# Half-size block products at the end of each MLP chunk, and their sums moved to GpSimd

## The chip, the core and the metric

The kernel runs on one core of a Trainium2 chip. The metric is the device time of one execution in microseconds (us), median of the runs shown; smaller is better. The profile calls the engines PE (TensorE matmuls), PEld (TensorE weight loads), DVE (VectorE), ACT (ScalarE), POOL (GpSimd) and SP (SyncE, which here issues nearly all DMAs).

## The reference

Two layers of a residual network on 1024 tokens of 1024 features. Each layer is a mixing part (a gated delta rule in layer 0, attention in layer 1), an MLP, and a gated projection. The change lies in the MLP:

```
hn = rms_norm(h, ln_mlp[layer])
h = h + jnp.square(jax.nn.relu(hn @ w_mlp1[layer])) @ w_mlp2[layer]
```

`w_mlp1` is 1024 x 4096 and `w_mlp2` 4096 x 1024, all float32. "First product" is `hn @ w_mlp1`, "second product" the one with `w_mlp2`.

## The kernel before

**Matmuls.** Every float32 operand is split in two parts of a reduced format, hi (an ACT cast) and lo (raw minus hi, one DVE `tensor_tensor`), by `split`, profile lines L224 and L225. `mm3` makes one product of three matmuls: hi·hi, hi·lo, lo·hi. All go through `Ordered.matmul`, L78. The weight block is the stationary side (128 x 128), the activations the moving side, up to 512 columns (half the tokens).

**First product.** The 4096 hidden features are cut into 8 chunks of 512. A chunk is a 2 x 2 block product (512 inputs twice, 256 features twice, 512 tokens twice), made as seven block products instead of eight, with sums of blocks before and after (Winograd's form of Strassen's method). Each block product is `product`: two raw weight tiles are split, then 2 x 4 x 3 = 24 matmuls of 512 columns. `front(c)` makes two of the seven, `rest(c)` five, in this order: weight blocks a21 with t3, a11 with t2, a22 with t4, s1 with t1, and last a12 with b22. t1 to t4 and b22 are sums and parts of the normalized activations, made once in each layer by `operands`, `make_t4` and `make_t1`: DVE sums (L283), ACT casts, DVE lo parts. The last block product adds onto the PSUM tiles that s1·t1 left (`ps`), after DVE has read them for g22; then g12 = u + ps. The fronts of chunks 0 to 3 come ahead of `operands`; `rest(c)` is followed by `front(c + 2)` for c = 2 to 5, so chunks 0, 1, 6 and 7 have no front behind them.

**After it.** ACT makes relu and square (L349, L350). The second product is made by the same method and needs sums of g11 to g22: before the change six DVE operations at the end of each chunk (g2 = g11 + g12, then g22 - g2 and g21 - g2, each for two tiles). `save` writes seven arrays of the chunk to DRAM (`gd`), from where the second product (`product2`) loads them.

**Tiles.** Raw weight tiles come from a ring of 8 (`raw`), split weight tiles from a ring of 12 (`w`), PSUM tiles for products from 8 banks in turn.

**Order.** The kernel's text gives priorities; a scheduler then sets the order on each engine with its own timeline of the program, and each engine executes its queue strictly in that order. So instructions of neighbouring products can stand interleaved, and an instruction that waits holds up all behind it on its engine.

Of the kernel before, what the change touches and what calls it, by code (L numbers as in the profile page):

```python
# [11 lines left out]
F32 = mybir.dt.float32  # L12
F32R = mybir.dt.float32r
# [103 lines left out]
class Trunk:  # L117
# [157 lines left out]

    def mlp(self, x, x_tags, gain, w1, w2, gain_next, h_dram, p, last):
        nc = self.nc
# [4 lines left out]
        def tt(out, a, b, op):  # L282
            nc.vector.tensor_tensor(out, a, b, op)  # L283
            return out

        def large(tags):
            hi, lo = (self.slot(t, [P, 4, HT], F32R, "t") for t in tags)
            return [(hi[:, k], lo[:, k]) for k in range(4)]

        def operands():  # L290
# [20 lines left out]
            def make_t1():  # L311
                b22.extend(self.split(x22[k], *self.hs_parts(1, 4 + k)) for k in range(4))
                return [self.split(t1s[k], *t) for k, t in enumerate(large((x_tags[0][1], x_tags[1][1])))]

# [113 lines left out]
        if self.unsquared:  # L428
            for i, a in enumerate(self.unsquared):
                self.add_square(1, a, marks[i // 4])  # L430

            def sums():
# [4 lines left out]
            front(1, amid=sums)  # L437
            self.pe.floor = self.pe.mark
# [143 lines left out]
    def split_p(self, p):  # L582
# [1452 lines left out]
def trunk(tc, x, p, ln_mix_e, w_in_e, gmlp_v_gain, gmlp_ws, gmlp_bs, gdn_conv, gdn_a_log, gdn_dt_bias, gdn_out_gain,  # L2035
          w_out_e, ln_mix_o, w_qkv_o, attn_q_gain, attn_k_gain, diff_lambda, attn_sub_gain, w_out_o, ln_mlp, w_mlp1,
          w_mlp2, ln_ple, w_ple_gate, w_ple_proj, masks, out):
    with ExitStack() as ctx:
# [54 lines left out]
        for layer in range(2):  # L2093
# [68 lines left out]
```

## Time and profile before

| | |
|---|---|
| median of 3 runs | 2481.62 us (2481.59 to 2485.3) |
| span of the profiled execution, first to last instruction | 2479.0 us (no other time of that execution is listed; the median is 2.6 us above it) |
| busy share PE / PEld / DVE / ACT / POOL | 99% / 85% / 75% / 52% / 13% |
| granted TensorE clock | 1.000 |
| first products of the MLPs | about 450 to 782 us (layer 0) and about 1725 to 2060 us (layer 1) |

"Busy" is the time in which an engine had an instruction in work. A row of the timeline gives start, duration, engine, line, operation, result and operands, shape, and in brackets the idle time before it with what ended it. A row of the windows gives a stretch of the span and in it the busy time of PE, PEld, DVE, ACT and POOL with instruction counts, the granted clock, the DMA share and GB/s. A row of the groups gives all instructions of one line and shape: busy time, mean ns of one, idle time before them.

### The profile page before, as it was taken

To read this page: it belongs to the slowest core of one execution; us is meant where nothing else is said; L and a number is where in the kernel's file an instruction comes from. 1 tells how busy PE (TensorE), PEld (TensorE's weight loads), DVE (VectorE), ACT (ScalarE), POOL (GpSimd) and SP (SyncE) were. 2 spreads that over 40 slices of the span, in tenths; PEclk is the share of its full clock that TensorE was granted. 3 is DMA by queue.
4 is the path that set the end of the run, shared out by engine and by line. 5 is a ranking of instruction groups with operands and counts; after the bars stand their busy time and mean duration, and the time that the engine had idled before them with its cause. 6 is when DMAs were issued, how large, how long until landed. Compare 5 with 4: busy or idle time off the path is not lost.

```text
span 2479.0 us, 39877 instructions
## 1 busy us (share of the span) xinstructions
PE 2463.4 (99%) x13597; PEld 2103.6 (85%) x13597; DVE 1863.9 (75%) x3638; ACT 1289.7 (52%) x2593; POOL 316.8 (13%) x296
## 2 busy tenths in 40 slices
PE   9999999999999999999999999999999999999999
PEld 7898898888888887888899999988878888878887
DVE  7787776697676879566568888876886677788687
ACT  6543444565445434454366666664755455445543
POOL 0221221000000000000244443441000000000010
PEclk9999999999999999999999999999999999999999
DMA  8475645457557756553347776787475558657872
GB/s 252 121 247 124 179 150 164 141 194 235 162 176 256 242 179 198 187 172 111 115 109 165 165 168 154 192 223 236 140 232 189 177 187 283 212 184 218 230 246 87
DMA packets 537748, 458.55 MB, mean 185 GB/s; under 512 B 228932, under 2 KB 399176, under 8 KB 537544
## 3 DMA queue, kind: packets, MB, share of 16 engines
q1 hardware_dynamic: 507192, 450.75, 59.7%
q10 hardware_dynamic: 29584, 3.68, 1.0%
q8 instruction: 107, 1.75, 0.3%
q0 software_dynamic: 768, 1.57, 0.2%
q14 instruction: 97, 0.79, 0.1%
HBM read 321.51 MB, written 134.37 MB: 184 GB/s over the span
## 4 chain that ended last, share of the span: by engine, by line
PE 94%; DVE 2%; DMA 2%; ACT 1%; issue 1%; POOL 0%; SPq 0%; DVEq 0%; ACTq 0%; POOLq 0%
PE mm L78 83%; PE po L78 3%; PE qk L78 3%; PE aux L78 2%; PE tr L81 1%; DMA spill<-early 0%; DMA aT<-a_dram 0%; PE pz L78 0%; DVE w L225 0%; PE pvn L78 0%; DMA diag<-early 0%; PE py L78 0%; PE aux L81 0%; PE pks L78 0%; PE pkq L78 0%
## 5 line engine op out<-in xcount | busy, mean ns | idle before, releaser
L78 PE MATMUL mm<-g,w 128*128 128x512 f32 x2592 | 603.5, 394 | 1.3 <-DVE g L225 0.7
L224 ACT CAST w<-raw 128x512 fp32r<-128x512 f32 x598 | 364.6, 616 | 444.1 <-PE mm L78 368.2
L78 PEld LDWEIGHTS mm<-g,w 128*128 128x128 f32 x2592 | 486.2, 188 | 116.3 <-DVE g L225 1.6
L78 PE MATMUL mm<-hi,w 128*128 128x512 f32 x1728 | 551.3, 396 | 0.0
L78 PE MATMUL mm<-w,hi 128*128 128x256 f32 (+2 forms) x2528 | 502.5, 294 | 0.7 <-ACT t L1587 0.7
L225 DVE TENSOR_TENSOR w<-raw,w 128x512 fp32r<-128x512 f32 (+1 forms) x510 | 348.2, 690 | 161.4 <-ACT w L224 150.1
L78 PEld LDWEIGHTS mm<-w,hi 128*128 128x128 f32 x2528 | 401.0, 188 | 15.5 <-ACT t L1587 0.9
L78 PEld LDWEIGHTS mm<-hi,w 128*128 128x128 f32 x1728 | 323.8, 188 | 73.4
L78 PE MATMUL mm<-w,lo 128*128 128x256 f32 (+2 forms) x1264 | 367.7, 292 | 0.0
L78 PE MATMUL mm<-lo,w 128*128 128x512 f32 x864 | 340.0, 394 | 0.0
L78 PE MATMUL mm<-t,w 128*128 128x512 f32 x1152 | 270.6, 394 | 0.2 <-DVE t L225 0.2
L78 PEld LDWEIGHTS mm<-t,w 128*128 128x128 f32 x1152 | 216.2, 188 | 51.3 <-DVE t L225 1.1
L78 PEld LDWEIGHTS mm<-w,lo 128*128 128x128 f32 x1264 | 237.8, 188 | 5.8
L78 PEld LDWEIGHTS mm<-lo,w 128*128 128x128 f32 x864 | 162.5, 188 | 36.3
L224 ACT CAST g<-graw 128x512 fp32r<-128x512 f32 x216 | 132.7, 617 | 44.6 <-DMA graw<-gd 16.3
L225 DVE TENSOR_TENSOR g<-graw,g 128x512 fp32r<-128x512 f32 x216 | 147.4, 687 | 10.2 <-DMA gd<-g 7.3
L1069 ACT ACTIVATE lg<-lg,nm 128x384 f32<-128x384 f32 (+7 forms) x128 | 99.2, 775 | 82.6 <-DVE nm L1066 81.8
L265 POOL TENSOR_TENSOR r<-ms,mhalf 128x4 f32<-128x4 f32 x12 | 12.5, 1043 | 940.2 <-DVE ms L263 915.8
L225 POOL TENSOR_TENSOR w<-raw,w 128x512 fp32r<-128x512 f32 (+1 forms) x88 | 113.8, 1313 | 133.3 <-ACT w L224 93.4
L349 ACT ACTIVATE g<-g 128x512 f32<-128x512 f32 x96 | 60.5, 631 | 112.3 <-DVE g L283 102.4
L1066 DVE CUSTOM_DVE_ANT_0 lg<-qk,al 128x512 f32<-128x512 f32 (+3 forms) x128 | 74.4, 585 | 25.0 <-PE qk L78 21.1
L78 PE MATMUL mm<-ohi,w 128*128 128x512 f32 x256 | 87.4, 402 | 1.5 <-ACT ohi L1142 1.1
(340 smaller groups left out, 3534.9 us busy)
## 6 DMA issues: line engine op xcount, KB each, us to landing
raw<-in_w_mlp_dram SPq DMA_DIRECT2D x352, 256.0 KB, 3.5
graw<-gd SPq DMA_DIRECT2D x224, 256.0 KB, 2.9
gd<-g SPq DMA_DIRECT2D x192, 256.0 KB, 3.2
raw<-in_w_ple_gate_dram SPq DMA_DIRECT2D x76, 256.0 KB, 3.7
acc<-h_dram SPq DMA_DIRECT2D x64, 256.0 KB, 4.3
keep<-in_w_mlp_dram SPq DMA_DIRECT2D x64, 256.0 KB, 4.5
raw<-in_w_in_e_dram SPq DMA_DIRECT2D x60, 256.0 KB, 3.8
h_dram<-acc SPq DMA_DIRECT2D x48, 256.0 KB, 2.2
```

Of the source, the lines that this page charges most:

```text
L78: self._next(self.engine.matmul(*a, **k))
L81: self._next(self.engine.transpose(*a, **k))
L224: self.nc.scalar.copy(hi, src)
L225: (lo_engine or self.nc.vector).tensor_tensor(lo, src, f32(hi), ALU.subtract)
L265: nc.gpsimd.tensor_tensor(r, ms, self.mhalf[:, 0:4], ALU.pow)
L349: nc.scalar.activation(g, src, AF.Relu)
L1066: nc.vector.tensor_tensor_reduce(out=lg[:, k0:k1], in0=ps[:, : k1 - k0], in1=al[:, u0 + k0 : u0 + k1], scale=-1.0, scalar=3.0e38 if c == 0 ...
L1069: nc.scalar.activation(lg[:, :n], lg[:, :n], AF.Exp, bias=nm[:, r, nch - 1 : nch], scale=-1.0, accum_out=me.sums[:, b, r : r + 1])
```

## The change

The last block product of each chunk, a12·b22, is now itself made by the seven-product method on halves (256 inputs, 128 features, 256 tokens): `blocks`. Seven half-size products of 2 x 3 matmuls with 256 columns, 42 matmuls, take the place of 24 with 512 columns.

- Sums of the weight block (s12, s4 and a new half of a0): four POOL operations on 256 elements, in two more tiles of the raw ring; then four splits (three of 512 columns, one of 256) instead of two.
- Sums of b22, once in each layer: y1 to y4, four POOL operations of 512 columns, ahead of the other operands; their lo parts on POOL as well (two of 256 columns, three of 512), their casts on ACT.
- Four of the seven products go to two PSUM tiles of their own (p16, and p57 in halves); DVE adds them to u (four additions of 256 columns, two of 512, one operand in PSUM); the others add onto `ps` as before. The second product into p16 adds onto the first, after DVE has read it.
- The six sums for the second product at the end of each chunk move from DVE to POOL, in place of g12, so the first waits until g12 has been saved.
- The four raw tiles of `split_p` come from the raw ring instead of the pool `tmp`.

```
-    def mlp(self, x, x_tags, gain, w1, w2, gain_next, h_dram, p, last):
+    def mlp(self, x, x22s, x_tags, gain, w1, w2, gain_next, h_dram, p, last):
+        def sums(out, a, b, op):
+            nc.gpsimd.tensor_tensor(out, a, b, op)
+            return out
+        L, R = slice(0, 256), slice(256, 512)
...
+            sums(y1, x22s[:, k1, R], x22s[:, k1, L], ALU.subtract)
+            sums(y2, x22s[:, k2, R], y1, ALU.subtract)
+            sums(y3, x22s[:, k2, R], x22s[:, k1, R], ALU.subtract)
+            sums(y4, x22s[:, k2, L], y2, ALU.subtract)
+            for k in range(2):
+                self.split(y1[:, k], *(y[:, R] for y in b22[k]), nc.gpsimd)
...
+        def blocks(raws, b, ps, u):
+            a0, a1 = raws
+            lo, hi = slice(0, P), slice(P, 2 * P)
+            s12, s4 = self.raw(2, 256), self.raw(2, P)
+            sums(s12[:, :, lo], a0[:, :, hi], a1[:, :, hi], ALU.add)
+            sums(a0[:, :, hi], a0[:, :, lo], a0[:, :, hi], ALU.subtract)
+            sums(s12[:, :, hi], s12[:, :, lo], a0[:, :, lo], ALU.subtract)
+            sums(s4, a1[:, :, lo], s12[:, :, hi], ALU.subtract)
+            a0, a1, s12, s4 = (self.parts(x, nc.vector) for x in (a0, a1, s12, s4))
...
+            sub(p16, a0, lo, b[1, 1], True)
+            tt(u0[:, L], u0[:, L], p16, ALU.add)
+            sub(ps[0][:, L], a1, lo, b[2, 1])
+            sub(ps[1][:, L], a1, hi, b[4])
+            sub(p5, s12, lo, b[1], True)
+            for x in u:
+                tt(x[:, R], x[:, R], p5, ALU.add)
+            sub(p16, s12, hi, b[2])
+            tt(u0[:, R], u0[:, R], p16, ALU.add)
+            tt(u1, u1, both(p16), ALU.add)
+            sub(p7, a0, hi, b[3], True)
+            tt(u1, u1, both(p7), ALU.add)
+            sub(ps[0][:, R], s4, slice(0, P), b[2, 2])
...
-            product(a12, b22, ps)
+            blocks(a12, halves, ps, u)
...
-                tt(g2[i], g11[i], g12[i], ALU.add)
-            save(6, c, g2)
+                sums(g12[i], g11[i], g12[i], ALU.add)
+            save(6, c, g12)
-                tt(g22[i], g22[i], g2[i], ALU.subtract)
-                tt(g21[i], g21[i], g2[i], ALU.subtract)
+                sums(g22[i], g22[i], g12[i], ALU.subtract)
+                sums(g21[i], g21[i], g12[i], ALU.subtract)
```

What stands on the engines. First POOL, from the end of layer 0's mixing part on (r is the norm's factor, al belongs to the attention of layer 1, hundreds of us later). Before:

```order
L1900 TENSOR_TENSOR fo_5236<-so_5231,mhalf 128x4
L1906 TENSOR_TENSOR qkv_2530<-qkv_2530,qkv_701 128x4x128
L265 TENSOR_TENSOR r_5175<-ms_5173,mhalf 128x4
L265 TENSOR_TENSOR r_5796<-ms_5794,mhalf 128x4
L920 IOTA al_12490 128x1024
L921 AFFINE_SELECT al_12490<-al_12490 128x1024
```

Now (y are the sums of b22, lo their parts, raw_6372 is s12, raw_6366 a0 and raw_6373 s4 of chunk 0):

```order
L265 TENSOR_TENSOR r_5796<-ms_5794,mhalf 128x4
L287 TENSOR_TENSOR y_1074_6115<-acc_5498 128x512
L225 TENSOR_TENSOR lo_6108<-y_1074_6115,hi_6107 128x256
L225 TENSOR_TENSOR lo_6110<-y_1074_6115,hi_6109 128x256
L287 TENSOR_TENSOR y_6116<-acc_5498,y_1074_6115 128x512
L287 TENSOR_TENSOR y_6117<-acc_5498 128x512
L287 TENSOR_TENSOR y_6118<-acc_5498,y_6116 128x512
L287 TENSOR_TENSOR raw_6372<-raw_6366,raw_6368 128x2x128
L287 TENSOR_TENSOR raw_6366<-raw_6366 128x2x128
L287 TENSOR_TENSOR raw_6372<-raw_6372,raw_6366 128x2x128
L287 TENSOR_TENSOR raw_6373<-raw_6368,raw_6372 128x256
L225 TENSOR_TENSOR y_6313<-y_6116,y_6312 128x512
```

POOL had nothing to do during the first product; it now has thirteen operations at its start, two of which follow the last row shown. Next DVE at the end of chunk 0 (u and g as above, v is there g2, w are lo parts of weight blocks, s the sum s1). Before:

```order
L283 TENSOR_TENSOR g_6107<-u_5705,mm_6310 128x512
L283 TENSOR_TENSOR v_6115<-g_5707,g_6107 128x512
L225 TENSOR_TENSOR w_6518<-raw_6427,w_6517 128x512
L283 TENSOR_TENSOR g_6111<-g_6111,v_6115 128x512
L283 TENSOR_TENSOR g_6109<-g_6109,v_6115 128x512
L283 TENSOR_TENSOR g_6108<-u_5706,mm_6311 128x512
L225 TENSOR_TENSOR w_6558<-s_1141_6420,w_6557 128x512
```

Now:

```order
L283 TENSOR_TENSOR u_5705<-u_5705,mm_6394 128x256
L225 TENSOR_TENSOR w_6504<-raw_6483,w_6503 128x512
L283 TENSOR_TENSOR u_5705<-u_5705,mm_6395 128x256
L283 TENSOR_TENSOR u_5706<-u_5706,mm_6395 128x256
L283 TENSOR_TENSOR raw_6661<-raw_6661,raw_6491 128x512
L225 TENSOR_TENSOR w_6536<-raw_6489,w_6535 128x512
L225 TENSOR_TENSOR w_6540<-raw_6491,w_6539 128x512
L225 TENSOR_TENSOR w_6574<-raw_6485,w_6573 128x512
L283 TENSOR_TENSOR u_5705<-u_5705,mm_6394 128x256
L283 TENSOR_TENSOR u_5706<-u_5706,mm_6394 128x512
L283 TENSOR_TENSOR g_6127<-u_5705,mm_6332 128x512
```

The sums v and g - v are gone from DVE, the additions of PSUM tiles to u have come, with the splits of the next chunk's blocks between them. Last PE at the same place: mm_6310 (before) and mm_6332 (now) are `ps`, mm_6394 is p16, mm_6395 p57, mm_6447 and mm_6507 belong to the next chunk's first product. Before:

```order
L78 MATMUL mm_6448<-lo_6083,w_6443 128x512
L78 MATMUL mm_6310<-hi_6276,w_6350 128x512
L78 MATMUL mm_6310<-lo_6277,w_6350 128x512
L78 MATMUL mm_6310<-hi_6276,w_6351 128x512
L78 MATMUL mm_6310<-hi_6280,w_6350 128x512
```

Now:

```order
L78 MATMUL mm_6395<-hi_6109,w_6387 128x256
L78 MATMUL mm_6507<-hi_6068,w_6499 128x512
L78 MATMUL mm_6507<-lo_6069,w_6499 128x512
L78 MATMUL mm_6508<-hi_6068,w_6499 128x512
L78 MATMUL mm_6508<-lo_6069,w_6499 128x512
L78 MATMUL mm_6332<-hi_6111,w_6382 128x256
L78 MATMUL mm_6332<-lo_6112,w_6382 128x256
L78 MATMUL mm_6332<-hi_6111,w_6383 128x256
```

Matmuls of 256 columns have taken the place of those of 512, and products of the next chunk stand between them.

More of the change, by code (lines that the diff above doesn't have):

```diff
@@ L311, in make_t1 @@
             def make_t1():
[L312 to L313 removed]
+                for k in range(4):
+                    cols = slice(0, 256 if k < 2 else 512)
+                    self.split(x22[k][:, cols], *(y[:, cols] for y in b22[k]))
+                out = [self.split(t1s[k], *t) for k, t in enumerate(large((x_tags[0][1], x_tags[1][1])))]
+                halves.update({(1, 1): [[y[:, L] for y in b22[k]] for k in (0, 1)], (2, 1): [[y[:, L] for y in b22[k]] for k in (2, 3)],
+                               (2, 2): [[y[:, R] for y in b22[k]] for k in (2, 3)], 1: [[y[:, R] for y in b22[k]] for k in (0, 1)]})
+                for n, y in ((2, y2), (3, y3), (4, y4)):
+                    if n < 4:
+                        ys = [self.tp.tile([P, 2, 256], F32R, tag="t", name=self.nm("y")) for _ in range(2)]
+                    else:
+                        ys = [self.sp.tile([P, 2, 256], F32R, tag=t, name=self.nm("y"), bufs=1) for t in ("sqs1", "rb1")]
+                    self.split(y, *ys, nc.gpsimd)
+                    halves[n] = [[z[:, k] for z in ys] for k in range(2)]
+                return out
             return t3, t2, make_t4, make_t1
@@ L343, in product, with sub, both @@
             return ps
+        def blocks(raws, b, ps, u):
[7 more added lines that the diff above has]
+            a0, a1, s12, s4 = (self.parts(x, nc.vector) for x in (a0, a1, s12, s4))
+            p16, p57 = (self.mm_ps() for _ in range(2))
+            p16, p5, p7 = p16[:, L], p57[:, L], p57[:, R]
+            def sub(out, w, cols, y, new=False):
+                for k in range(2):
+                    self.mm3(out, [z[:, k, cols] for z in w], y[k], new and k == 0, k == 1, not new)
+            def both(p):
+                return p.unsqueeze(1).to_broadcast([P, 2, 256])
+            u0, u1 = u
+            sub(p16, a0, lo, b[1, 1], True)
+            tt(u0[:, L], u0[:, L], p16, ALU.add)
+            sub(ps[0][:, L], a1, lo, b[2, 1])
+            sub(ps[1][:, L], a1, hi, b[4])
+            marks.append(self.pe.mark)
+            sub(p5, s12, lo, b[1], True)
+            for x in u:
+                tt(x[:, R], x[:, R], p5, ALU.add)
+            sub(p16, s12, hi, b[2])
+            u1 = u1.rearrange("p (h t) -> p h t", h=2)
+            tt(u0[:, R], u0[:, R], p16, ALU.add)
[3 more added lines that the diff above has]
+            sub(ps[0][:, R], s4, slice(0, P), b[2, 2])
+            marks.append(self.pe.mark)
         def tiles(tags, name):
@@ L376, in rest @@
             g12, g21, g22 = (tiles((f"c{8 + 2 * i}", f"c{9 + 2 * i}"), "g") for i in range(3))
-            v, g2 = ([self.sp.tile([P, HT], F32, tag=f"{n}{h}", name=self.nm("v"), bufs=1) for n in ("sqs", "rb")] for h in range(2))
+            v = [self.sp.tile([P, HT], F32, tag=f"{n}0", name=self.nm("v"), bufs=1) for n in ("sqs", "rb")]
             s1 = self.slot("B", [P, 2, 2, 256], F32, "s1")
@@ L435, in sums @@
                 self.pe.floor = self.pe.mark
-            front(1, amid=sums)
+            front(1, amid=squares)
             self.pe.floor = self.pe.mark
```

13 lines of the change are left out of this document (9 added, 4 removed).

## The prediction

> **What bounds the kernel now.** I read the page's busy shares and its chain of waits first, then the chain in order of time for the stages of the change.
>
> ```profile
> span 2479.0 us, 39877 instructions
> PE 2463.4 (99%) x13597; PEld 2103.6 (85%) x13597; DVE 1863.9 (75%) x3638; ACT 1289.7 (52%) x2593; POOL 316.8 (13%) x296
> ...
> PE 94%; DVE 2%; DMA 2%; ACT 1%; issue 1%; POOL 0%; SPq 0%; DVEq 0%; ACTq 0%; POOLq 0%
> ```
>
> PE is the bound: 94% of the chain is matmuls. In the chain the pitch of the matmuls can be read off unbroken runs (start, us, what), and a view of the groups in the second run's stretch shows which matmuls it holds:
>
> ```profile
> 488.22 290.34 PE mm L78 x1254
> ...
> 1358.99 5.66 PE mm L78 x48
> ```
>
> ```profile
> L78 PE MATMUL mm<-w,hi 128*128 128x256 f32 x32 | 5.7, 281 | 0.0
> L78 PE MATMUL mm<-w,lo 128*128 128x256 f32 x16 | 4.5, 280 | 0.0
> ```
>
> With 512 columns one matmul takes 290.34 / 1254 = 231.5 ns of PE's time, with 256 columns, each with a weight block of its own, 5.66 / 48 = 117.9 ns. So the first run shows layer 0's first product without a gap. That doesn't mean that nothing else is near. The windows over the start of both layers' `rest` chunks, and over two chunks in the middle and one late one, show DVE beside it (third busy figure):
>
> ```profile
> 488.00:508.00 20.00, 20.00 (x89) 16.25 (x89) 19.60 (x32) 15.44 (x29) 0.00 (x0) 1.00 0.31 95
> 508.00:528.00 20.00, 20.00 (x88) 16.27 (x87) 20.00 (x35) 14.04 (x26) 0.00 (x0) 1.00 0.52 169
> 528.00:548.00 20.00, 20.00 (x89) 16.23 (x88) 16.40 (x27) 8.44 (x15) 0.00 (x0) 1.00 0.68 220
> 548.00:571.00 23.00, 23.00 (x101) 18.72 (x100) 20.63 (x34) 12.66 (x23) 0.00 (x0) 1.00 0.72 239
> 1769.00:1789.00 20.00, 20.00 (x88) 16.19 (x88) 20.00 (x33) 15.49 (x29) 0.00 (x0) 1.00 0.40 134
> 1789.00:1809.00 20.00, 19.80 (x85) 15.53 (x84) 20.00 (x35) 10.41 (x19) 0.00 (x0) 1.00 0.39 120
> 1809.00:1829.00 20.00, 20.00 (x88) 16.17 (x87) 18.36 (x32) 12.92 (x23) 0.00 (x0) 1.00 0.87 279
> 1829.00:1849.00 20.00, 20.00 (x88) 16.24 (x88) 15.07 (x25) 9.47 (x16) 0.00 (x0) 1.00 0.77 260
> ```
>
> ```profile
> 610.00:649.00 39.00, 39.00 (x170) 31.70 (x169) 24.73 (x40) 20.28 (x36) 0.00 (x0) 1.00 0.53 176
> ...
> 727.00:755.00 28.00, 28.00 (x123) 22.75 (x122) 19.28 (x31) 12.98 (x23) 0.00 (x0) 1.00 0.48 161
> ```
>
> Where the operands t1 to t4 are made, DVE is full for 40 us in each layer, and PE lives on what DVE has just finished. The timeline shows how close:
>
> ```profile
> 517.06 0.69 DVE L225 TENSOR_TENSOR w<-raw,w 128x512 fp32r<-128x512 f32 x1
> 517.66 0.70 DVE L283 TENSOR_TENSOR raw<-s,raw 128x512 f32<-128x512 f32 x1
> ```
>
> ```profile
> 517.91 0.41 PEld L78 LDWEIGHTS mm<-hi,w 128*128 128x128 f32 x2
> ...
> 1801.84 5.39 PEld L78 LDWEIGHTS mm<-t,w 128*128 128x128 f32 x24 [0.46 <-DVE t L225]
> 1807.85 0.76 PEld L78 LDWEIGHTS mm<-t,w 128*128 128x128 f32 x4 [0.62 <-DVE t L225]
> ```
>
> By the order on both engines, the lo part that DVE ends at 517.75 is the first of chunk 0's a21, and the weight load at 517.91 is the one that takes it: a lead of 0.16 us. In layer 1 PE already waits for DVE's t twice. DVE starts a new operation every 0.60 us there (517.06, 517.66).
>
> **The change part by part.** PE: per chunk 24 x 231.5 = 5556 ns go and 42 x 117.9 = 4952 ns come, 604 ns less; 16 chunks give 9.7 us. This lies on the path.
>
> POOL gets, per layer, four operations of 512 columns and two of 256 at once when the activations are normalized, then four of 256 and three of 512; and per chunk four of 256 and six of 512. Beside POOL lies DVE, and the trace shows what they do to each other:
>
> ```profile
> 388.20 1.29 POOL L1906 TENSOR_TENSOR qkv<-qkv,qkv 128x512 f32<-128x512 f32 x1 [1.65 <-ACT qkv L1903]
> ...
> 424.42 1.30 POOL L1906 TENSOR_TENSOR qkv<-qkv,qkv 128x512 f32<-128x512 f32 x1 [2.15 <-ACT qkv L1903]
> ```
>
> ```profile
> 388.68 1.35 DVE L248 TENSOR_TENSOR sqs<-sqs,t 128x512 f32<-128x512 f32 x1
> ...
> 424.90 1.37 DVE L248 TENSOR_TENSOR sqs<-sqs,t 128x512 f32<-128x512 f32 x1 [0.83 <-ACT t L245]
> ```
>
> ```profile
> L248 DVE TENSOR_TENSOR sqs<-sqs,t x70: 647/687/1367, 383.5 to 2388.2; 128x512 f32<-128x512 f32 x70
> ```
>
> This DVE addition takes 0.687 us in the median, but 1.35 and 1.37 where a POOL operation was in work. Taking 0.69 off its end, it began to work at 389.34 and 425.58: 1.14 and 1.16 us after POOL's start. So a POOL operation of 512 columns holds up a DVE operation with two SBUF inputs for 1.15 us. A DVE operation with one input in PSUM isn't held:
>
> ```profile
> 237.98 1.28 POOL L1906 TENSOR_TENSOR qkv<-qkv,qkv 128x512 f32<-128x512 f32 x1 [0.40 <-ACT qkv L1903]
> ```
>
> ```profile
> 238.31 0.69 DVE L1868 TENSOR_TENSOR qkv<-po,carved 128x512 f32<-128x512 f32 x1 [0.67 <-PE po L78]
> ```
>
> Prices of the rest, from the groups:
>
> ```profile
> L225 POOL TENSOR_TENSOR w<-raw,w 128x512 fp32r<-128x512 f32 x84 | 110.9, 1340 | 127.5 <-ACT w L224 87.7 <-PE mm L78 39.5
> ...
> L225 POOL TENSOR_TENSOR w<-raw,w 128x256 fp32r<-128x256 f32 x4 | 3.0, 740 | 5.7 <-ACT w L224 5.7
> ```
>
> ```profile
> L283 DVE TENSOR_TENSOR g<-u,mm 128x512 f32<-128x512 f32 x64 | 43.8, 685 | 18.1 <-PE mm L78 18.0
> ...
> L963 DVE TENSOR_TENSOR q<-mm,ssf 128x256 f32<-128x256 f32 x32 | 13.4, 418 | 5.5 <-POOL ssf L959 5.0
> ```
>
> For POOL's 256 columns no row shows a block; I take 740 less the 0.14 us by which POOL outlasts its hold above, 0.60. Its bounds are 0 and 0.74.
>
> The Trainium skill (page "SBUF — State Buffer", section "Who interferes with whom") says that a VectorE instruction with two SBUF inputs and a GpSimd instruction that reads SBUF exclude each other, whichever starts first holding the port for its whole instruction. The two rows agree in kind; for the whole instruction the holds would be 1.30 and 0.74, and the sum below about 4 us higher.
>
> Layer 0, opening: 4 x 1.15 + 2 x 0.60 = 5.8 us of holds between 491 and 517, where every DVE operation has two SBUF inputs. Two lo parts of b22 are only half as wide now: 2 x (0.69 - 0.42) = 0.5 back. Less the lead of 0.16, PE waits 5.1 us. Next group: 4 x 0.60 + 3 x 1.15 = 5.85 against 3.6 us in which DVE idles up to 548: 2.3. Chunk 1: the ten operations of a chunk hold 4 x 0.60 + 6 x 1.15 = 9.3 us; about a third of DVE's operations there read PSUM and pass, which leaves 6.2, against 2.4 idle and a lead that grows again behind 571; I take 1. Together 8.4 us.
>
> Layer 1: DVE has no idle time from 1769 to 1809 and PE no lead, so both groups count in full, 5.8 - 0.5 + 5.85 = 11.1. The first chunk's 6.2 meet 1.6 + 4.9 us of idle: 0.
>
> Chunks 2 to 7: DVE idles 14.3 us in a chunk with a front (39 - 24.73) and 8.7 without (28 - 19.28), against holds of 9.3. DVE's own work stays: six sums go, 6 x 0.69 = 4.1; 0.69 + 0.42 for two splits, 4 x 0.42 and 2 x 0.69 for additions come, 4.2. On average this fits; for bursts I take 1 us per layer, 2 in all (bounds 0 and 16, 1 us in each chunk).
>
> ACT gets 43 more instructions, casts like these:
>
> ```profile
> L224 ACT CAST w<-raw 128x512 fp32r<-128x512 f32 x598 | 364.6, 616 | 444.1 <-PE mm L78 368.2
> ```
>
> They lie in its idle time (4.6 us of 488 to 508, 6.0 of the next 20); were they late, the y parts would be. PE needs those for chunk 0's a12, which stands 116 matmuls behind the first of a21: 517.0 + 116 x 0.2315 = 544. The added wait on POOL (the first sum behind the save of g12) has the next chunk's s4 behind it, needed some 20 us later. SP's saves now wait for POOL, about 8 us of operations, with weight loads queued behind:
>
> ```profile
> L283 DVE TENSOR_TENSOR raw<-raw,raw 128x512 f32<-128x512 f32 x64 | 44.0, 693 | 32.4 <-DMA raw<-in_w_mlp_dram 32.3
> ```
>
> DVE already waits for these loads, 32.4 us over 64, half a microsecond each, without PE feeling it; I cost them at nothing, and leave their worst case to the 16 us above. The p loads, now in the raw ring, come at a chunk's end; 0, at most a landing of 3.4 us:
>
> ```profile
> t<-in_p_dram SPq DMA_DIRECT2D x8, 256.0 KB, 3.4
> ```
>
> Sum: -9.7 + 8.4 + 11.1 + 2 = +11.8. On the profiled span 2479.0 + 11.8 = 2490.8; the median stands 2.6 above the span: 2493.
>
> **The rivals.** Only the first six POOL operations are felt, the rest falls where DVE waits or reads PSUM: 5.1 + 5.3 - 9.7 = +0.7, 2482. For it speaks DVE's idle time in 528 to 548; against it, layer 1 has none until 1809.
>
> Faster: DVE isn't held (the long rows at 388 and 424 have another cause), and POOL runs beside it. Then PE's saving is left: 2481.6 - 9.7 = 2472. It decides once all stalls together stay under 4.7 us. Against it stand two rows that end alike to 0.02 us after POOL's start.
>
> POOL starves: DVE, back to back, keeps the port, and POOL's thirteen opening operations, 7 x 1.34 + 6 x 0.74 = 13.8 us, come only when DVE first idles:
>
> ```profile
> 544.21 0.69 DVE L225 TENSOR_TENSOR w<-raw,w 128x512 fp32r<-128x512 f32 x1 [1.19 <-ACT w L224]
> ```
>
> The half products then start at 543.0 + 13.8 = 557 instead of 544: 13 us in each layer, 2481.6 - 9.7 + 26 + 2 = 2500. Against it, POOL got the port behind a single DVE operation (1.88 us instead of about 1.3, the DVE operation ending at 87.45):
>
> ```profile
> 86.73 1.88 POOL L1556 TENSOR_TENSOR z<-z,carved 128x512 f32<-128x512 f32 x1 [5.66 <-DVE z L1555]
> ```
>
> ```profile
> 86.71 0.74 DVE L1514 SCALAR_TENSOR_TENSOR t<-cx,cols,t 128x512 f32<-128x512 f32 x1
> ```
>
> Every chunk late: DVE's additions of p16 arrive late because POOL holds the splits ahead of them, 1 us in each of 16 chunks: 2493 - 2 + 16 = 2507. PE's order has up to 24 half and 6 whole matmuls (4.2 us) between the two products into p16, which speaks against more.
>
> That the smaller matmuls save nothing would need a pitch of 5556 / 42 = 132 ns; the 48 above show 118.
>
> **How the numbers follow.** My forecast, 2493, has 0.50 (own range 2485 to 2503); the first rival 0.20, faster 0.12, starving 0.08, every chunk late 0.10. Two tenths of a percent, 5 us, is about what a measurement can tell from no change: slower 0.50 + 0.08 + 0.10 = 0.68, same 0.20, faster 0.12. The range leaves out the faster case and the edges: 2479 to 2510.
>
> **What would show it.** Right: POOL rows inside 490 to 530 with DVE rows of 1.2 us and more beside them, PE idle by DVE some 5 to 8 us in layer 0 and 9 to 13 in layer 1, 256-column matmuls at 118 ns. Wrong: DVE rows at 0.69 beside POOL's, or PE without gaps there.

## The result, and the profile after

The changed kernel takes 2509.12 us (2507.38 to 2512.09, 4 runs) against 2481.77 for the kernel before beside it: ratio 1.0109, 95% interval 1.0095 to 1.0124. It is slower, as forecast and inside the range, but by 27.4 us where the forecast had 11.4. The profiled execution spans 2506.3 us (2479.0 before).

The page after: busy time of the engines, and the shares of the chain of waits.

```profile
PE 2465.1 (98%) x13885; PEld 2115.4 (84%) x13885; DVE 1928.9 (77%) x3670; ACT 1309.2 (52%) x2635; POOL 567.9 (23%) x474
...
PE 84%; DVE 7%; DMA 4%; issue 3%; ACT 1%; POOL 1%; SPq 0%; DVEq 0%; POOLq 0%; ACTq 0%
```

PE has fallen from 94% of the chain to 84%. The windows show where (busy time of PE, PEld, DVE, ACT, POOL, then the granted clock): both openings, and a middle chunk without loss.

```profile
488.00:508.00 20.00, 17.22 (x77) 13.74 (x77) 19.60 (x24) 12.36 (x25) 9.32 (x6) 1.00 0.13 41
508.00:528.00 20.00, 18.82 (x81) 14.84 (x80) 20.00 (x34) 15.16 (x27) 0.00 (x0) 1.00 0.43 145
...
548.00:571.00 23.00, 21.80 (x109) 18.34 (x109) 22.90 (x33) 12.31 (x22) 11.22 (x9) 1.00 0.71 235
...
727.00:755.00 28.00, 28.00 (x125) 22.77 (x124) 21.27 (x31) 12.67 (x23) 12.82 (x10) 1.00 0.46 152
...
1803.00:1823.00 20.00, 15.25 (x62) 11.29 (x62) 17.93 (x31) 12.49 (x24) 11.51 (x4) 1.00 0.31 105
```

What ended PE's idle time (total, times, longest); before, no wait of this kind was over 1 us in the MLPs:

```profile
PE mm L78 <- DVE g L225: 6.7, 5, 2.2
PE mm L78 <- DVE g L283: 6.1, 5, 2.6
PE mm L78 <- DVE w L225: 4.3, 8, 1.2
PE mm L78 <- ACT w L224: 4.0, 2, 3.6
PE mm L78 <- ACT u L432: 3.0, 2, 2.8
```

"DVE g L225" is the second product: its first operands come late. No term of the forecast was there.

PE's saving itself came. The first matmuls on y in the half products of chunks 2 to 4 (each chunk has them at the same place):

```profile
609.22 1.57 PE L78 MATMUL mm<-y,w 128*128 128x256 f32 x12
...
648.20 0.99 PE L78 MATMUL mm<-y,w 128*128 128x256 f32 x7
...
686.50 1.22 PE L78 MATMUL mm<-y,w 128*128 128x256 f32 x9
```

A chunk now lasts 38.30 us (686.50 - 648.20), as 144 x 231.5 + 42 x 117.9 ns = 38.29; before, 168 x 231.5 = 38.89.

The clock is new. The last columns of a window's row are the granted clock, DMA share and GB/s:

```profile
817.00:820.00 3.00, 3.00 (x9) 2.33 (x8) 1.24 (x3) 1.14 (x2) 0.00 (x0) 0.50 0.88 255
...
1823.60:1827.00 3.40, 3.06 (x9) 2.27 (x8) 3.40 (x6) 0.98 (x2) 0.00 (x0) 0.50 0.24 77
1868.00:1871.40 3.40, 3.40 (x12) 2.80 (x11) 3.40 (x7) 2.67 (x5) 2.18 (x3) 0.50 0.61 232
```

Three times in the MLPs the clock is 0.50 for 3.41 us, each time right behind a gap of PE of 2.2 to 3.6 us. That is 3 x 1.7 us of lost matmul time in which PE counts as busy. Before, the MLPs ran at 1.00 throughout.

So the 27.3 us between the two spans add up as follows. A gap costs 0.27 us more than its length, start to start: at 507.42 PE starts 3.17 us behind the matmul before it and the next comes after 0.33, which is 3.04 over two pitches for a gap of 2.78.

| where | gaps, us | with 0.27 each and the half clock |
|---|---|---|
| PE's saving | | -9.7 |
| layer 0, 488 to 571 | 5.9 in 4 | 7.0 |
| layer 0, 571 to 620 | 3.2 in 4 | 4.2 |
| layer 0, last chunk and start of the second product | 4.5 in 4 | 5.6 + 1.7 |
| layer 1, 1782 to 1825 | 5.4 in 6 | 7.0 + 1.7 |
| layer 1, 1825 to 1910 | 3.3 in 3 | 4.1 + 1.7 |
| layer 1, last chunk and start of the second product | 3.7 in 3 | 4.5 |
| sum | | 27.8 |

The sum comes within 0.5 us of the spans, but two errors in it partly cancel. PE's matmuls on `aux` stand ahead of and behind each MLP's stages of the table. In layer 0 they start at 477.7 and 1021.6 us before and at 477.9 and 1035.5 now, so that 13.7 us are lost between them, and the table has 13.7 as well. In layer 1 they start at 1760.5 and 2303.6 before and at 1775.2 and 2330.9 now, a loss of 12.6 us, where the table has 14.2. About 1.2 us more come between the two MLPs, with a gap of 1.13 us at 1744 that the table leaves out.

### The profile page after: what moved, and what is told of

Same layout as the page of the kernel before. It is cut to its first block, busy times and chain, and to the rows that moved or that the text cites. A ratio compares the mean times of both kernels' runs of the same rounds, so it can differ in the third digit from the quotient of the medians.

```text
span 2506.3 us, 40925 instructions
## 1 busy us (share of the span) xinstructions
PE 2465.1 (98%) x13885; PEld 2115.4 (84%) x13885; DVE 1928.9 (77%) x3670; ACT 1309.2 (52%) x2635; POOL 567.9 (23%) x474
## 4 chain that ended last, share of the span: by engine, by line
PE 84%; DVE 7%; DMA 4%; issue 3%; ACT 1%; POOL 1%; SPq 0%; DVEq 0%; POOLq 0%; ACTq 0%
PE mm L78 72%; PE po L78 3%; PE qk L78 3%; PE aux L78 2%; DVE w L225 1%; DMA gd<-g 1%; DMA raw<-in_w_mlp_dram 1%; DVE raw L283 1%; PE tr L81 1%; DMA keep<-in_w_mlp_dram 1%; POOL g L287 1%; DVE u L283 1%; DVE acc L283 0%; DVE g L283 0%; DVE acc L1431 0%
## 5 line engine op out<-in xcount | busy, mean ns | idle before, releaser
L224 ACT CAST w<-raw 128x512 fp32r<-128x512 f32 (+1 forms) x630 | 381.2, 611 | 404.8 <-PE mm L78 319.9
L78 PE MATMUL mm<-hi,w 128*128 128x512 f32 (+1 forms) x1728 | 523.1, 381 | 18.6 <-DVE g L283 5.9
L225 DVE TENSOR_TENSOR w<-raw,w 128x512 fp32r<-128x512 f32 (+2 forms) x542 | 385.2, 716 | 175.6 <-ACT w L224 139.8
L78 PEld LDWEIGHTS mm<-hi,w 128*128 128x128 f32 x1728 | 315.0, 189 | 85.2 <-DVE g L283 7.4
L78 PE MATMUL mm<-lo,w 128*128 128x512 f32 (+1 forms) x864 | 326.2, 378 | 0.7 <-DVE lo L225 0.7
L287 POOL TENSOR_TENSOR g<-g,g 128x512 f32<-128x512 f32 x96 | 146.1, 1542 | 91.0 <-DMA gd<-g 48.7
L224 ACT CAST g<-graw 128x512 fp32r<-128x512 f32 x216 | 132.6, 617 | 52.5 <-DMA graw<-gd 18.1
L225 DVE TENSOR_TENSOR g<-graw,g 128x512 fp32r<-128x512 f32 x216 | 149.1, 695 | 9.9 <-POOL g L287 8.0
L265 POOL TENSOR_TENSOR r<-ms,mhalf 128x4 f32<-128x4 f32 x12 | 12.6, 1047 | 628.4 <-DVE ms L263 602.2
L225 POOL TENSOR_TENSOR w<-raw,w 128x512 fp32r<-128x512 f32 (+1 forms) x88 | 113.8, 1313 | 133.3 <-ACT w L224 92.6
L287 POOL TENSOR_TENSOR raw<-raw,raw 128x256 f32<-128x256 f32 x48 | 59.0, 1229 | 285.8 <-DVE raw L283 188.1
```

Source lines behind the costliest of these rows:

```text
L78: self._next(self.engine.matmul(*a, **k))
L224: self.nc.scalar.copy(hi, src)
L225: (lo_engine or self.nc.vector).tensor_tensor(lo, src, f32(hi), ALU.subtract)
L265: nc.gpsimd.tensor_tensor(r, ms, self.mhalf[:, 0:4], ALU.pow)
L287: nc.gpsimd.tensor_tensor(out, a, b, op)
```

## The experiments

Each version was compared with the kernel before on the same chip, whose median lay between 2480.7 and 2481.8. "+" is the difference of the medians to it. "Hold" is worked out from the rows: what DVE's two-input operations with 512 (256) columns take beyond 0.685 (0.415) us, summed over those that are more than 0.15 us over.

**What of the change costs: one part at a time.**

`sum_into_g11` and `g_sums_vector`: the second product's six sums, into a tile that is free, on GpSimd or on VectorE.

```diff
-                sums(g12[i], g11[i], g12[i], ALU.add)
-            save(6, c, g12)
+                sums(g11[i], g11[i], g12[i], ALU.add)     # g_sums_vector: tt for all three lines
+            save(6, c, g11)
-                sums(g22[i], g22[i], g12[i], ALU.subtract)
-                sums(g21[i], g21[i], g12[i], ALU.subtract)
+                sums(g22[i], g22[i], g11[i], ALU.subtract)
+                sums(g21[i], g21[i], g11[i], ALU.subtract)
```

> The changed kernel, but GpSimd's first sum of the second product's operands is written into g11 (dead after its save) and no longer into g12, so it need not wait until the save of g12 has landed. Theory A (the wait for the landing, 2.2 to 5.8 us at the end of the last chunk, and the saves and loads queued behind it, make the second product start late): the PE gaps there (2.2 and 1.1 us in layer 0, 2.2 and 0.7 in layer 1) go, with the half-speed stretch that follows the one of layer 0, and part of the stalls of chunks 0 and 1: 2496 to 2501 us, 8 to 13 less than 2509. Theory B (GpSimd's slowness and its hold on VectorE are what counts): 2507 to 2509, the gaps stay within 0.5 us.

Measured: 2516.24 us, +34.8, ratio 1.0139 (1.0120 to 1.0159). Theory A, which I held then, falls: without the wait for the landing the kernel is no faster. Its four runs lie between 2508.6 and 2522.9 us, so that slower by 7 us isn't shown. The sums come earlier, at 560.92 instead of 564.20, and PE has gaps of 3.6 us at 580 and 2.4 at 621, each with a half-speed stretch.

> The changed kernel with the six sums of the second product's operands back on VectorE, written into g11. Theory A (the wait for the save's landing): the same as with the sums into g11 on GpSimd within 3 us, 2494 to 2501. Theory B (GpSimd's slowness and hold): 2494 to 2499, and 8 us and more below the version with the sums into g11 on GpSimd. If neither, and the stalls are those of the operands made at the opening alone: 2505 to 2509.

Measured: 2490.37, +8.9, ratio 1.0033 (1.0021 to 1.0045). Moving these six sums back takes 18.7 of the 27.4 us away. The gap at the start of layer 0's second product is gone, in layer 1 0.5 us is left, and from 571 on no chunk has a gap.

`y_vector`: the y sums and y lo parts on VectorE. `blocks_vector`: the four sums of a chunk's blocks on VectorE. In both, `sums` becomes `tt` in those lines.

```diff
-            sums(y1, x22s[:, k1, R], x22s[:, k1, L], ALU.subtract)    # y_vector, and y2 to y4
+            tt(y1, x22s[:, k1, R], x22s[:, k1, L], ALU.subtract)
-                    self.split(y, *ys, nc.gpsimd)
+                    self.split(y, *ys)
-            sums(s12[:, :, lo], a0[:, :, hi], a1[:, :, hi], ALU.add)  # blocks_vector, and the other three
+            tt(s12[:, :, lo], a0[:, :, hi], a1[:, :, hi], ALU.add)
```

> The changed kernel with the four y sums and the lo parts of y on VectorE. By the hold theory a POOL operation of the opening costs VectorE 0.55 to 1.1 us (3.6 in all by its long rows at 496 to 501 in layer 0), and on VectorE the same sums take 4 x 0.69 + 2 x 0.41 = 3.6: the opening's first stall stays within 1 us of 2.8 us, and the time within 3 us of 2509. Rival (GpSimd is starved by VectorE and late with y, so that the half products wait): 2500 to 2505. Rival (no hold worth the name; the rows are long for another reason): 2512 to 2518, since VectorE then has 3.6 + 2.9 us more to do where it is full.

Measured: 2506.69, +25.3, ratio 1.0102 (1.0088 to 1.0116), 2.4 less than the changed kernel: within what the hold theory allows, and not the 2512 and more of "no hold". The single gaps don't fit so well: layer 0's of 2.8 us is gone, and one of 2.05 at 522 stands in its place.

> The changed kernel with the four sums of each chunk's blocks on VectorE, the g sums and y left on GpSimd. Hold theory: each of the four 128x256 sums held VectorE 0.4 to 0.6 us and takes it 0.41 itself: within 3 us of 2509. Rival (their lateness on GpSimd, one took 5.89 us, is what makes the half products wait): 2500 to 2505.

Measured: 2498.55, +17.8, ratio 1.0072 (1.0059 to 1.0085): 10.6 less than the changed kernel, more than either theory had. This row of the changed kernel speaks for lateness: a sum that takes 0.74 us alone starts when DVE runs back to back, and ends six microseconds later.

```profile
528.39 5.89 POOL L287 TENSOR_TENSOR raw<-raw,raw 128x256 f32<-128x256 f32 x1 [26.65 <-ACT t L224]
```

In layer 1 the same sum takes 9.48 us. In both layers it ends 0.6 us after DVE has stopped for want of the cast that follows on the sum (at 533.7 and 1820.2 us), and in layer 1 PE's longest gap, 3.6 us, ends on that cast ("ACT w L224" above):

```profile
1811.33 9.48 POOL L287 TENSOR_TENSOR raw<-raw,raw 128x256 f32<-128x256 f32 x1 [15.21 <-ACT g L417]
```

```profile
1822.30 0.69 DVE L225 TENSOR_TENSOR w<-raw,w 128x512 fp32r<-128x512 f32 x1 [2.07 <-ACT w L224]
```

That was the rival "POOL starves", in small. The parts don't add: 18.7 + 10.6 + 2.4 is 32, and all together bring 16.7 (`all_vector`, below). They share the same stalls.

**Is it the hold, or what waits for the sums?** `before_g12_pool` is the kernel before with the six sums alone on GpSimd, as the change has them. `six_idle_sums` leaves the real sums on VectorE and adds six on GpSimd that nothing waits for.

```diff
-                tt(g2[i], g11[i], g12[i], ALU.add)                        # before_g12_pool
-            save(6, c, g2)
+                nc.gpsimd.tensor_tensor(g12[i], g11[i], g12[i], ALU.add)  # and the other four
+            save(6, c, g12)
```

```diff
             save(6, c, g2)                                                # six_idle_sums
+            idle = self.slot("d0", [P, HT], F32, "idle")
+            nc.gpsimd.tensor_tensor(idle[:, 0:4], g12[0][:, 0:4], g12[1][:, 0:4], ALU.subtract)
+            for i in range(6):
+                nc.gpsimd.tensor_tensor(idle, f32(b11[i % 4][0]), f32(b11[(i + 1) % 4][0]), ALU.add)
```

> The kernel before with one part of the change alone: the six sums of the second product's operands on GpSimd, the first in place in g12. Theory A (late saves and late start of the second product by the wait in place): 2489 to 2494, 7 to 12 above 2481.8, with gaps of 2 us at the start of the second product of both layers. Theory B (what costs is the work at the opening and in the half products): 2481 to 2484.

> The kernel before (its own sums on VectorE, where they were), with six GpSimd additions of 128x512 per chunk more, started by a sum of 4 columns of g12; they read b11 and write a tile that nothing reads, so no save, load or sum waits for them. Theory B (GpSimd's reading of SBUF holds up VectorE's own work, and that is what the six sums on GpSimd cost): long VectorE rows of some 25 us in all in the first product of each layer as with the real sums, and 2488 to 2493. Theory E (the lateness of the sums, of their saves and of what stands behind these in SP's queue): 2481 to 2484.

Measured: 2491.61, +10.2, ratio 1.0036 (1.0024 to 1.0049), and 2492.78, +12.1, ratio 1.0044 (1.0031 to 1.0056). Sums for which nothing waits cost as much as the real ones. So the hold is enough for a loss of this size, and theory E isn't needed for it. That lateness has no part in the real sums' 10.2 us isn't shown, since the idle ones hold DVE half as long again (below). The time of `before_g12_pool` lies in theory A's range, but not for A's reason: no gap of PE stands at the start of its second product. So the sums on GpSimd don't by themselves make the second product late. VectorE's lines of `six_idle_sums` in layer 0's first product (min/median/max in ns):

```profile
L225 DVE TENSOR_TENSOR w<-raw,w x86: 675/687/1784, 488.0 to 778.1; 128x512 fp32r<-128x512 f32 x86
```

```profile
L283 DVE TENSOR_TENSOR raw<-raw,raw x32: 675/692/1785, 511.8 to 753.0; 128x512 f32<-128x512 f32 x32
L283 DVE TENSOR_TENSOR g<-u,mm x30: 671/680/689, 533.5 to 782.9; 128x512 f32<-128x512 f32 x30
```

The longest row with two SBUF inputs has 1.1 us more than the median; of the 30 with one input in PSUM ("mm") none is long. The hold from 547 to 642 us is 18.4 us in 18 rows here, 12.4 in 13 in `before_g12_pool`, 12.1 in 14 in the changed kernel, 2.4 in 6 with the sums on VectorE, and 0 in the kernel before.

**The hold by itself.** Four sums, or eight memsets, on GpSimd at the opening; nothing reads what they write.

```diff
             t1s = []                                                          # of the kernel before
+            y = self.slot("c12", [P, HT], F32, "y")                           # four_idle_sums
+            for k in range(4):
+                nc.gpsimd.tensor_tensor(y, x22[k], x22[(k + 1) % 4], ALU.subtract)
+            nc.gpsimd.tensor_tensor(y[:, 0:4], x22[0][:, 0:4], x22[1][:, 0:4], ALU.subtract)  # eight_idle_memsets instead
+            for k in range(8):
+                nc.gpsimd.memset(y, 0.0)
```

> The kernel before, with four GpSimd subtractions of 128x512 (x22 less x22) per layer added where the changed kernel makes its y sums; nothing reads their result. Hold theory: VectorE rows of 1.2 to 1.8 us beside them instead of 0.69, 3 to 4.6 us in all, and PE waits as much within the next 30 us: 3 to 4.5 us per layer, 2487 to 2491. Rival (no hold): 2481 to 2483 and VectorE rows at 0.69.

> The kernel before, with a GpSimd subtraction of 4 columns and eight GpSimd memsets of 128x512 (about 0.53 us each, 4.2 in all) per layer at the same place; they write SBUF and read none of it. If it is the reading of SBUF that holds VectorE: VectorE rows at 0.69 and 2481 to 2483. If any GpSimd work on SBUF does: as with the four sums, 2486 and more.

Measured: 2493.89, +12.8, ratio 1.0042 (1.0028 to 1.0056), and 2481.06, ratio 1.0002 (0.9993 to 1.0010). POOL's rows and DVE's beside them, the sums first, then the memsets:

```profile
499.40 3.35 POOL L304 TENSOR_TENSOR y<-acc 128x512 f32<-128x512 f32 x2 [0.70 <-DVE acc L1367]
```

```profile
499.78 1.80 DVE L283 TENSOR_TENSOR acc<-acc,acc 128x512 f32<-128x512 f32 x1
501.50 1.80 DVE L283 TENSOR_TENSOR s<-raw,raw 128x512 f32<-128x512 f32 x1
```

```profile
495.72 4.62 POOL L305 MEMSET y<- 128x512 f32 x8
```

```profile
498.11 0.68 DVE L283 TENSOR_TENSOR acc<-acc,acc 128x512 f32<-128x512 f32 x1
498.72 0.68 DVE L283 TENSOR_TENSOR s<-raw,raw 128x512 f32<-128x512 f32 x1
```

Sums that read SBUF hold DVE here; memsets, which only write it, don't. The Trainium skill ("SBUF — State Buffer", section "Who interferes with whom") says that a VectorE instruction with two SBUF inputs contends with a GpSimd instruction that reads SBUF and not with one that only writes it; these runs agree. I had 2487 to 2491 for the four sums. PE's gaps were as expected, 3.4 us in each layer. What came on top is one half-speed stretch in layer 0 and two, 6.8 us, in layer 1.

**SP's queue.** SP's own waits in the changed kernel, 540 to 640 us: the saves (L421) wait for POOL, with weight loads behind them.

```profile
SPq L421 <- POOL g L287: 16.8, 16, 3.8
```

`saves_on_pool` takes these saves out of SP's queue.

```diff
-        def save(n, c, g):
+        def save(n, c, g, queue=nc.sync):
             for i in range(2):
-                nc.sync.dma_start(gd[n - 1][c][i], g[i])
+                queue.dma_start(gd[n - 1][c][i], g[i])
...
-            save(6, c, g12)          # and save(4, c, g22), save(5, c, g21)
+            save(6, c, g12, nc.gpsimd)
```

> The changed kernel with the saves of the six sums (three pairs of a chunk) issued by GpSimd behind its own sums, and no longer by SP. Theory C (the saves stand in SP's queue waiting for GpSimd, 16.8 us of the stretch 540 to 640, and hold up the weight loads behind them): most of what the sums on GpSimd cost goes, 2489 to 2496; SP's waits for POOL are 0. Theory B' (GpSimd's hold on VectorE and the lateness of its results, not the queue): 2503 to 2511.

Measured: 2556.71, +75.6, ratio 1.0301 (1.0287 to 1.0315): neither theory. SP's saves wait for POOL no more (from 540 to 640 us 3.8 us of SP's waits for POOL are left, all at loads, L522), but now POOL keeps DVE away for far longer:

```profile
569.25 0.65 POOL L421 DMA_DIRECT2D gd<-g  x1
569.93 2.56 POOL L287 TENSOR_TENSOR g<-g,g 128x512 f32<-128x512 f32 x2
572.43 0.57 POOL L421 DMA_DIRECT2D gd<-g  x1
573.02 2.56 POOL L287 TENSOR_TENSOR g<-g,g 128x512 f32<-128x512 f32 x2
```

```profile
569.79 6.35 DVE L283 TENSOR_TENSOR raw<-raw,raw 128x512 f32<-128x512 f32 x1
```

One DVE operation took 6.35 us: four sums with saves between them went ahead of it, where without the saves sums and DVE's operations take turns. So this run doesn't tell what the queue costs. In the changed kernel the chain does pass through it once: the weight load below is issued only behind a save (at 600.93) that waited for the sum above it. DVE waits for this load, and behind it does the g for which PE waits 1.42 us at 605.

```profile
599.60 1.31 POOL g L287
...
601.34 3.60 DMA raw<-in_w_mlp_dram
```

So the queue has a part there. How much in all stays open; `six_idle_sums`, in which no save waits for POOL, shows that a loss of the size of the six sums' doesn't need it.

**Where PE's 9.7 us go without GpSimd.** `all_vector` has g sums (into g11), y and block sums all on VectorE.

> The changed kernel with every sum and lo part that it gave to GpSimd on VectorE (g sums into g11): the half-size products alone. If the parts add up: 2490.4 (g sums on VectorE) less 2.4 (y on VectorE) less 0 to 4 for the sums of the blocks, 2484 to 2488, and no VectorE row beside POOL is longer than 0.8 us. If PE's saving of 9.7 us comes through, VectorE having room: 2472 to 2478. If VectorE becomes the bound in the chunks (6.6 us more per chunk than GpSimd left it): 2492 and more.

Measured: 2492.39, +11.3, ratio 1.0043 (1.0031 to 1.0056), no long DVE row. The time lies in the third range, but not for that range's reason: in chunks 1 to 6 no gap is over 0.5 us. The loss is in two places: the opening, 2.05 us in layer 0 and 3.1 in layer 1, where DVE had no room, and the start of the second product, 2.6 and 3.1. Three half-speed stretches go with them. The chain at layer 0's second product:

```profile
791.90 0.42 SPq L352
...
792.37 5.43 DMA acc<-h_dram
...
797.81 3.89 DMA graw<-gd
801.70 0.69 DVE g L225
```

The following versions build on it, each with the edits of the one before.

```diff
+            queue = nc.gpsimd if c == NCH - 1 and n in (1, 6, 4, 5) else nc.sync   # vector_late_saves, in save
-        ps = product2(1, beside={8: (1, 0)})
+        ps = product2(1, beside={12: (1, 0)})
-            tt(y1, x22s[:, k1, R], x22s[:, k1, L], ALU.subtract)        # vector_late_y: from operands
+                tt(y1, x22s[:, k1, R], x22s[:, k1, L], ALU.subtract)    # to make_t1; so y2 to y4, then the splits
-                if n == 1 and kt < 4:      # vector_free_slots
-                    b = self.hs_parts(0, 4 + kt)
+                if n == 1 and kt < 8:
+                    b = self.hs_parts(0, (4 + kt) % 8)
+            if last:                       # free_slots_layer0; no y in layer 1
+                product(a12, b22, ps)
```

> The version with every sum on VectorE (2492.4), and two things more: the last chunk's saves 1, 6, 4 and 5 are issued by GpSimd, which does nothing else there, so that the loads of the second product don't stand behind them in SP's queue, and the 1 MB of h for the first half is fetched four steps later. If the second product's late start (gaps of 2.6 and 3.1 us and two half-speed stretches of 1.7 us) comes from that queue and that fetch: 2482 to 2485. If the memory's rate is the bound there whatever the order: 2490 to 2493.

Measured: 2489.25, +8.5, ratio 1.0032 (1.0019 to 1.0044): 3 us less than `all_vector`, about a third of what I expected. Gaps of 0.9 and 2.0 us are left at the second product.

> As the one before, and the y sums and their splits are written behind the splits of b22 in make_t1, instead of ahead of t4: the gaps of the opening (2.05 us in layer 0, 3.1 in layer 1, with a half-speed stretch) shrink below 1 us: 4 to 7 us less than the one before, 2476 to 2480. If VectorE is only late at another place (chunk 0's half products or chunk 1): within 2 us of the one before.

Measured: 2487.42, +6.7, ratio 1.0026 (1.0016 to 1.0035). Layer 0's opening gap of 2.05 us is down to 0.18, and three more of 0.2 to 0.4 us, 0.9 together, stand at 544 to 547. In layer 1 it is split in five small ones, 4.6 us together, and the half-speed stretch there is gone. 1.8 us less, not 4 to 7.

> The version with every sum on VectorE, late y and late saves (2487.4), and in the second product the split parts of operands 4 to 7 are put into the place of b11, which is free, instead of the slots of u and g of the last chunk. If the gap at the start of the second product (1.3 us in layer 0, 1.7 in layer 1) is the wait for the last chunk's saves to give these slots free: the gaps go, 2483 to 2485. If it is the landing of the g loads themselves: gaps as before, 2486 to 2488.

Measured: 2482.32, +0.7, ratio 1.0006 (0.9997 to 1.0015). No gap at the second product any more, so it was the wait for the last chunk's saves, whose slots the operands took. What is left, at layer 1's opening:

```profile
PE mm L78 <- DVE t L225: 1.3, 1, 1.3
PE mm L78 <- ACT w L224: 1.3, 2, 0.9
PE mm L78 <- DVE y L225: 1.1, 1, 1.1
PE mm L78 <- DVE w L225: 0.9, 1, 0.9
```

> The same, with the half-size blocks in layer 0 alone; layer 1 makes the last block product of each chunk as the kernel before does, and no y. Layer 0 has gaps of 0.7 and 0 to 1.3 us against 4.85 saved, layer 1 loses nothing and saves nothing: 2477 to 2480. If layer 1's opening (4.6 us of gaps) isn't due to the y parts and half blocks: 2482 and more.

> The kernel before with the three edits at the second product alone (operands 4 to 7 in b11's place, the last chunk's saves 1, 6, 4 and 5 on GpSimd, h fetched four steps later). It has no gap there to lose: 2480 to 2483, so that a gain of the other two is the blocks'.

Measured: 2479.64, -2.0, ratio 0.9993 (0.9984 to 1.0002), and the control 2482.20, ratio 0.9999 (0.9990 to 1.0008). With the half blocks in layer 0 alone the kernel is at best 2 us faster than before, which the interval doesn't tell from nothing. Nor is it so that layer 1 loses nothing: PE has a gap of 1.13 us at 1733, ahead of layer 1's first product, where it waits for the norm's sum of squares (DVE sqs L248). All eleven versions with half-size blocks in chunk 0 of layer 0 have this gap, 1.13 to 1.17 us; the other eight profiles, the kernel before among them, have none there. In the eleven PE's order has 21 matmuls between the last transposes and the one that takes the squares, in the others 27. Why the scheduler sets it so is open.

`blocks_from_chunk2` and `blocks_from_chunk2_gated` leave the opening alone: chunks 0 and 1 use the old product, and y is made in chunk 1.

```diff
-            blocks(a12, halves, ps, u)
+            if c < 2:
+                product(a12, b22, ps)
+            else:
+                blocks(a12, halves, ps, u)
...
+            g = g[0][:, 0:8].rearrange("p (k t) -> p k t", k=2)   # gated: ahead of each y sum
+            tt(y[:, :, 0:4], g, g, SUB)
```

> As the version with free slots and every sum on VectorE (2482.3), but the half-size blocks are used in chunks 2 to 7 alone, and their y operands are made in chunk 1 from the split parts of x22, by 20 additions of 256 columns on VectorE, spread over three places of the chunk. The opening is then as before. If the opening was what took the saving: 12 chunks save 12 x 0.604 = 7.2 us, layer 1's gaps go, and 2474 to 2477 is left. If chunk 1 has no room for 11 us more on VectorE (it idles 25 us in 548 to 642 before): gaps there, 2478 to 2483.

> As blocks_from_chunk2, but each of the four y sums begins with an operation of 4 columns that reads a g tile of chunk 1 or 2, so that the scheduler can't move the sums forward into the opening, as it did there (VectorE rows on y from 499 us on, 2.9 us of gaps at 524, 2.7 at 1808). If the opening is what took the saving: no gaps up to 548 in layer 0 and none at 1808, 12 x 0.604 = 7.2 us saved, less up to 3 for chunk 1: 2474 to 2478. If chunk 1 has no room for 11 us on VectorE: gaps between 580 and 640, 2479 to 2484.

Measured: 2487.52, +6.0, ratio 1.0023 (1.0014 to 1.0032), and 2488.33, +6.6, ratio 1.0029 (1.0017 to 1.0040), both above all that was forecast for them. The first told nothing about chunk 1, since the scheduler moved the y sums into the opening. In the second the opening has no gap, but in both layers PE stops ahead of chunk 2's half-size products, 4.8 and 3.6 us, with 10.2 us at half speed. Its chain in layer 0:

```profile
593.75 0.70 DVE g L283
...
594.72 4.14 DMA raw<-in_w_mlp_dram
...
598.88 0.70 DVE raw L283
...
600.58 0.63 ACT w L224
```

A save waits in SP's queue for DVE's g, which stands behind the y sums, and the weight load behind that save is issued at 594.7; PE waits for its landing. So the opening isn't the only place without room: chunk 1 has 25 us of idle DVE time before the change, and can't take 11 us more as this version puts them there.

## Why the forecast was right, and where it was not

**PE's gain, -9.7:** right, 0.6 us in each chunk.

**The hold, 1.15 us of a POOL operation of 512 columns:** right in kind, and shown by the idle sums against the memsets. In `six_idle_sums` a held row is 1.02 us over (18.4 / 18), in the changed kernel 0.86 (12.1 / 14, its sums of 256 columns among them). The Trainium skill ("SBUF — State Buffer", section "SBUF: two separate sides") has whichever starts first keep the shared ports for its whole instruction. By that a held row would be an estimated 1.30 us over, the length of a POOL row; the rows stay below it. At layer 0's opening the rows look as foretold:

```profile
495.95 1.23 DVE L225 TENSOR_TENSOR w<-raw,w 128x512 fp32r<-128x512 f32 x1
497.10 1.78 DVE L283 TENSOR_TENSOR acc<-acc,acc 128x512 f32<-128x512 f32 x1
498.80 1.79 DVE L283 TENSOR_TENSOR s<-raw,raw 128x512 f32<-128x512 f32 x1
500.51 1.51 DVE L225 TENSOR_TENSOR lo<-acc,hi 128x256 fp32r<-128x256 f32 x1
```

**The openings, 8.4 - 1 and 11.1:** about right in size, 7.0 and 8.7 with the half clock in it, but in layer 1 by luck. There the holds left PE 1.3 us of gaps up to 1809, where I had 5.3 for the first group alone; the largest loss is the gap of 3.6 us and its half-speed stretch at 1822, which ended on the cast of the sum that took POOL 9.48 us. That is a rival's mechanism, and not that of my sum. (With every sum on VectorE, `all_vector`, layer 1 loses a gap of 3.1 us all the same, since DVE has no room.) In layer 0 the first stall is of the foretold kind, 2.8 us of PE for 3.8 of holds. PE waits through ACT first ("ACT u L432", 2.8 us), whose casts stand behind DVE's late sums; ACT at 0 was a path I had not followed.

**"Chunk 1: 9.3 us of holds, I take 1", and "on average this fits ... 2 in all": this step failed.** The holds came out smaller than I had them: 12.1 us from 547 to 642, where POOL works off the 30 operations of three chunks, so 4.0 in a chunk against 6.2. Wrong was to set them off against DVE's idle time. `six_idle_sums` shows the error's size: 12 us for sums that nothing needs, where my balance would have made them nearly free. It also shows two ways in which the balance fails. One is that the sums come in a burst and meet DVE where it has no idle time. The kernel before has such a stretch (third busy figure), and in `six_idle_sums` held rows fall into it, and PE's gap of 2.35 us at 571 ends a chain that from 555 us on is DVE's work without a load:

```profile
557.00:567.00 10.00, 10.00 (x45) 8.11 (x44) 10.00 (x18) 3.13 (x5) 0.00 (x0) 1.00 0.72 231
```

```profile
559.56 1.78 DVE v L283
561.34 1.70 DVE w L225
```

The other is that DVE's idle time lies in waits for work that hangs on DVE itself. From 540 to 790 us in the kernel before it waits 29.9 us for ACT's casts and 17.7 for weight loads, and SP waits to issue these loads until DVE has done a lo part (28.4 us of 540 to 640), which frees a raw tile. Time taken from DVE therefore comes back as a later load, as ahead of the gap of 1.49 us at 1892:

```profile
1884.90 0.61 DVE w L225
...
1885.52 3.60 DMA raw<-in_w_mlp_dram
```

In the changed kernel the chunks from 571 to 620 and 1825 to 1910 lost 10.0 us (1.7 of it the clock) against 3. How this divides between bursts, later loads and SP's queue isn't shown.

**Not in the sum: the last chunk and the second product's start,** 11.8 us (1.7 of it the clock). I had left SP's saves and the p loads at nothing and looked at the chunks only, and never at the stage that follows on the last chunk's saves. With the six sums on VectorE 0.5 us of gaps is left there. With half blocks and no GpSimd the gap came back; there the last chunk's saves hold slots that the second product wants (`vector_free_slots`). That they do so because the last chunk ends earlier is my reading and not shown.

**Not in the sum: the clock,** 5.1 us in all, which stand in the amounts above: a price on longer gaps.

**The rivals.** "DVE isn't held" is refuted. That only the opening's first six operations are felt falls with the 10.0 us in the chunks behind it. "POOL starves" happened, 5.9 us for one sum in layer 0 and 9.5 in layer 1, but its 13 us per layer at the half products did not come. "Every chunk late by 1 us", 2507, is nearest in time and wrong in place: from 617 and 1907 us on PE has no gap until the last chunk.

## What to carry over

GpSimd is not a free place for sums where VectorE works on two SBUF operands: a sum of 512 columns that meets such an operation takes about a microsecond from VectorE, more than the 0.69 us that it would cost there. A balance of busy and idle time over a whole chunk says little: work that comes in a burst meets the stretch without room, and idle time of an engine that waits for loads can't be spent, if it is that engine which frees the buffers of the next loads. When work at a stage's end moves to a slower engine, follow it into the next stage: slots and queue places held by the last saves decide when that begins.

## What was not expected of the hardware

A gap of PE costs more than its length. In the MLPs of all 19 profiles here, from the first products to the end of the second, 37 stretches of 3.41 us or two or three times that run at half clock, each at a gap of PE. All 17 gaps of 3 us and more had one, 16 of 32 between 1.7 and 3 us, and 4 of 47 between 1.0 and 1.7. These four are at one place, the gap of 1.13 to 1.17 us at the start of layer 1's first product. 3.41 us at half clock cost 1.7 us. The Trainium skill ("TensorE: Matmul & The Clock Gate", section "What's actually happening") has a free-running window of 3413 ns and half clock after at least one idle window of about 3.4 us. The length agrees; gaps of half a window, and four times of a third, were enough here, and below 3 us it was a matter of chance.

With POOL's DMA issues between its sums (`saves_on_pool`) 21 of DVE's `tensor_tensor` operations in the MLPs took 2.5 to 6.35 us; in the other 18 profiles none took over 1.9. Why the issues do this isn't shown. It also goes the other way: POOL's sum of 9.48 us, 0.74 alone, stood while 14 DVE operations began and ended.
